# The first two feed-forward units of the second layer as eight plain block products

## The chip, the cores and the metric

The kernel runs on one core of a Trainium2 chip. The metric is device time in microseconds (us), taken as the median of several executions; one further execution was recorded by the hardware profiler, and its trace is what is read here. TensorE (PE; its weight loads are PEld) multiplies, VectorE (DVE) and ScalarE (ACT) work element by element and read TensorE's results from PSUM, GpSimd (POOL) works element by element in SBUF, SyncE (SP) issues transfers.

## The reference, cut to what matters

Two layers of a diffusion backbone run over 640 tokens of width 1024: 512 latent tokens and 128 context tokens, each group with its own conditioning vector. A layer is attention and then a feed-forward network with hidden width 2816. All is float32. The part that the change touches is the feed-forward of the second layer:

```
h = rms_norm(x, norm_ffn) * (1.0 + sc_f) + sh_f          # 640 x 1024
gate, up = jnp.split(h @ w_gate_up, 2, axis=-1)          # each 640 x 2816
x = x + g_f * ((jax.nn.silu(gate) * up) @ w_down)
```

## The kernel before

**Layout.** The residual stream is held transposed: eight tiles x0 to x7 of 128 channels by 640 tokens. A product takes weights as the stationary operand and tokens as the moving one. Each float32 operand is split into a high part of reduced precision and a low remainder (hi and lo), and `prod` sums three matmuls for each pair of blocks of 128 channels: hi x hi, hi x lo, lo x hi (L662, L663, L664). Weights are split by `split`: ACT copies the high part (L87), VectorE subtracts it (L88). They lie in four buffers each, called whi and wlo, of 1024 columns; raw weights arrive in two raw buffers of 1 MB, loaded by SP. `w_next(ahead)` gives the next piece of a list of pieces (`specs`) and prepares so many more.

**The second layer's gate and up.** Layer 1 (counted from 0) is in `FAST`. There the token columns are cut in two halves of 320 (`HALVES`), the weights of two 128-row blocks and the eight channel blocks in two each, and the 2 x 2 x 2 block product is made with seven products in place of eight (Strassen's scheme in Winograd's form). Two units, one for gate and one for up, make two hidden blocks r = 0, 1 for both token halves c = 0, 1. One unit is seven products of four channel pairs, 7 x 4 x 3 = 84 matmuls of 128 x 320. The first of the three parts (`PARTS`, 8, 8 and 6 hidden blocks) thus has four pairs of units, and the whole layer eleven. After each part, `residual` multiplies by w_down.

The seven products pair a weight factor with a token factor:

```
    FACTORS = {"A11": "B11", "A12": "B21", "S2": "T2", "S1": "T1", "S3": "T3", "A22": "T4", "S4": "B22"}
```

A11 to A22 are blocks of the weights and S1 to S4 sums of them, made by GpSimd in `fast_prep` (L496 to L499) and split into half a whi and half a wlo buffer each. B11 and B21 are the normed tokens of the first half (channel blocks 0 to 3 and 4 to 7), B12 and B22 those of the second half, T1 to T4 sums of them. B12 itself is no factor. `fast_tiles` lays the 28 pairs of tiles for the seven factors into buffers called k, q, Q and V.

**The seam.** `residual` of the attention ends with the last three output blocks for the first half, then for the second. After each half `norm_stats` makes the sums of squares (L398), `rsqrt` a chain of nine tiny VectorE steps (L99 to L105), and two sets of matmuls spread the result (rstd) over the partitions (L402, tile rb). `fast_norm` scales the eight blocks on VectorE (L456) into tmp, a P buffer of which there are three. For the first half `split` adds the shift and cuts (L90 on ACT, L91 on VectorE) into B11 and B21. For the second half ACT adds the shift (L473); then `fast_norm` goes on at once, for each i of four, with B22 and the sums T3, T1, T2, T4 on VectorE (L477 to L486), and `cut` splits each (L443 on ACT, L444 on GpSimd). `fast_unit` then evacuates the products by ACT (L534) and VectorE (L522), gate applies Silu on ACT (L558), and up multiplies on GpSimd (L562).

**Order.** The program is handed to a planner which simulates the engines and fixes each engine's order of instructions from the order in the text (earlier is more urgent), the operands' readiness and the buffers' release. On the chip each engine then goes through its own list in that order and waits where an operand is late.

Of the kernel before, what the change touches and what calls it, by code (L numbers as in the profile page):

```python
# [12 lines left out]
F32R = mybir.dt.float32r  # L13
I32 = mybir.dt.int32
AF = mybir.ActivationFunctionType
ALU = mybir.AluOpType
# [3 lines left out]
P = 128  # L20
D = 1024
KC = D // P
DEPTH = 2
SEQ = 128
DEC = 512
NT = SEQ + DEC
# [9 lines left out]
HALF = NT // 2  # L36
HALVES = ((0, HALF), (HALF, NT))
FAST = (1,)
# [8 lines left out]
class Net:  # L47
# [398 lines left out]
    def fast_norm(self, state, half, rb):  # L446

        nc = self.nc
        v = nc.vector
        l, _, T, a = state  # L450
        g0, g1 = HALVES[half]
        segs = [(s, e, c) for s, e, c in ((g0, min(g1, DEC), 0), (DEC, g1, 1)) if s < e]

        def scaled(out, k):
            for s, e, c in segs:
                v.scalar_tensor_tensor(out[:, s - g0:e - g0], self.xT[k][:, s:e], a[:, k, c:c + 1],  # L456
                                       rb[:, s - g0:e - g0], ALU.mult, ALU.mult)

        n = KC // 2
        if half == 0:  # L460
            for name, k0 in (("B11", 0), ("B21", n)):
                for i in range(n):
                    tmp = self.t([P, HALF], "P", bufs=3)
                    scaled(tmp, k0 + i)
                    self.split(*T[name][i], tmp, bias=self.m(l, 3, k0 + i, 0))
            return
        for i in range(n):
            tmp = self.t([P, 2, HALF], "P", bufs=3)
            for j, k in enumerate((i, n + i)):
                scaled(tmp[:, j], k)  # L470
                for s, e, c in segs:
                    w = tmp[:, j, s - g0:e - g0]
                    nc.scalar.activation(w, w, AF.Identity, bias=self.m(l, 3, k, c))  # L473
            b12, b22 = tmp[:, 0], tmp[:, 1]
            self.cut(T["B22"][i], b22)
            t3 = self.fast_temp()
            v.tensor_tensor(t3, b22, b12, ALU.subtract)  # L477
            self.cut(T["T3"][i], t3)
            for part in T["B11"][i]:
                v.tensor_tensor(b12, b12, part.bitcast(F32), ALU.subtract)  # L480
            self.cut(T["T1"][i], b12)
            v.tensor_tensor(b22, b22, b12, ALU.subtract)
            self.cut(T["T2"][i], b22)
            t4 = self.fast_temp()
            v.tensor_tensor(t4, T["B21"][i][0].bitcast(F32), b22, ALU.subtract)
            v.tensor_tensor(t4, t4, T["B21"][i][1].bitcast(F32), ALU.add)  # L486
            self.cut(T["T4"][i], t4)
# [56 lines left out]
        self.fast_product(p3, T)  # L544
        out(0, 1, lambda o: add(o, p3, u))

    def fast_gate_up(self, T, n, act, side):

        nc = self.nc
        for i in range(0, n, 2):  # L550
            g = [self.t([P, NT], "P", bufs=3) for _ in range(2)]

            def part(r, c):
                return g[r][:, c * HALF:(c + 1) * HALF]

            def gate(r, c, add):
                o = add(part(r, c))
                nc.scalar.activation(o, o, AF.Silu)  # L558

            def up(r, c, add):  # L560
                x, o = add(self.fast_temp()), part(r, c)
                nc.gpsimd.tensor_tensor(o, o, x, ALU.mult)  # L562

            self.fast_unit(T, gate)
            self.step(side)
            self.fast_unit(T, up)
            for r in (1, 0):
                self.split(act[0][i + r], act[1][i + r], g[r])
            self.step(side)

    def norm_chunk(self, state, k, g0, g1, rb):
# [20 lines left out]
    def wstream(self):  # L592

        ins = self.ins
        specs = []

        def spec(key, src, n, parts, shape):
            for a, b in parts:
                specs.append((key, n, src, (a, b), shape))

        every, half = slice(0, None), [slice(0, P), slice(P, 2 * P)]
        for l in range(DEPTH):
            for i in range(0 if l else 2, len(self.blocks)):
                spec(("in", l, i), ins["w_in"][l, i], KC, [(slice(4 * j, 4 * j + 4), every) for j in range(2)], [4, 256])
            for i in range(4):
                spec(("out", l, i), ins["w_out"][l, i], KC, [(every, h) for h in half], [KC, P])
            j0 = 0
            for n in PARTS:
                if l in FAST:
                    for i, name in self.fast_order(n):  # L610
                        u, j = i % 2, j0 // 2 + i // 2
                        specs.append((("gu", l, u, j), KC, ins["w_gate_up"][l, u, j], name, None))
                else:
                    for j in range(j0 // 2, (j0 + n) // 2):
                        for h in half:
                            for u in range(2):
                                spec(("gu", l, u, j), ins["w_gate_up"][l, u, j], KC, [(every, h)], [KC, P])
                for i in range(4):
                    spec(("dn", l, j0, i), ins["w_down"][l, i, :, j0:j0 + n], n, [(every, h) for h in half], [n, P])
                j0 += n  # L620
        self.specs = specs
        self.raws, self.wt, self.pos, self.prepped, self.loaded = {}, {}, 0, 0, 0
        self.spare = None
# [528 lines left out]
    def ffn(self, l, h, side):  # L1152
        nc = self.nc
        nxt = None
        for pi, n in enumerate(PARTS):
            if pi == 2:
                while side:
                    self.step(side)
            if pi < 2 or l == DEPTH - 1:
                act = [[self.t([P, NT], f"{x}{j}", F32R) for j in range(n)] for x in ("hi", "lo")]  # L1160
            else:
                v = self.t([P, 6, NT], "V", F32R)
                act = [[self.t([P, NT], "Q", F32R, bufs=6) for _ in range(n)], [v[:, j] for j in range(n)]]
            if l in FAST:
                self.fast_gate_up(h, n, act, side)
            for j in range(0 if l in FAST else n):
                out = []
                for u in range(2):
                    w = self.w_next()
                    s, parts = self.acc2()  # L1170
                    for i in range(2):
                        self.prod(parts[i], self.columns(w, h, GROUPS[i], range(KC)))
                    out.append(s)
                    if u == 0:
                        sg = self.t([P, NT], "P", bufs=3)
                        nc.scalar.activation(sg, s, AF.Silu)
                        if pi or j > SKIP:
                            self.step(side)
                nc.vector.tensor_tensor(sg, out[1], sg, ALU.mult)
                self.split(act[0][j], act[1][j], sg)  # L1180
                if pi or j > SKIP:
                    self.step(side)
            if pi == len(PARTS) - 1 and l + 1 < DEPTH:
                nxt = (l + 1, 0)
            r = self.residual(l, act, 5, range(n), nxt, side)
        return r
# [92 lines left out]
```

## Time and profile before

| | us |
|---|---|
| median of 3 executions | 1732.97 |
| lowest and highest | 1732.89 and 1733.89 |
| the profiled execution, its own time | 1731.6 |
| its span, first to last instruction | 1729.8 |
| TensorE busy in it | 1659.9 |
| VectorE, ScalarE, GpSimd busy | 1184.7, 674.7, 469.4 |

The span is what the trace shows; the 1.8 us between it and the execution's own time lie outside the instructions. Busy time of TensorE is from modelled ends of pipelined matmuls, so how many matmuls a stretch holds says more than its busy share. The granted clock of TensorE has two levels, 1.2 and 2.4 GHz; 1.00 stands for the higher one.

### The profile page before, as it was taken

What the parts mean: (1) busy time and instruction counts of PE and PEld (TensorE: products, weight loads), DVE (VectorE), ACT (ScalarE), POOL (GpSimd) and SP (SyncE); (2) the same over time, 40 slices, a digit from 0 to 9 for tenths busy, and PEclk for the clock granted to TensorE, in tenths of its full rate; (3) what the DMA queues carried; (4) which work ended last, traced back from release to release, by engine and by line L of the source; (5) the groups of instructions that cost most, each with busy time, mean ns of one, the idle gap of its engine ahead of it and who ended that gap; (6) DMA issues with size and microseconds to landing.
All of it is one profiled execution on the core that took longest, in us unless ns stands there. A gap on an engine that the chain in (4) does not pass through costs nothing.

```text
span 1729.8 us, 29420 instructions
## 1 busy us (share of the span) xinstructions
PE 1659.9 (96%) x11934; PEld 1577.7 (91%) x11934; DVE 1184.7 (68%) x2019; ACT 674.7 (39%) x1309; POOL 469.4 (27%) x410
## 2 busy tenths in 40 slices
PE   8989889999999999999999999999959999999999
PEld 6869878898999999999989998888948999999998
DVE  5786667878588978722267875777488854883672
ACT  4433376733321122212245425766244432441440
POOL 0243534400000000000003364443056622741440
PEclk9989999998999999999999999999968999999999
DMA  9343211153265655321231202112101221222222
GB/s 343 120 161 106 56 25 32 44 197 120 66 215 171 200 178 186 106 89 59 89 113 54 79 17 52 34 53 74 49 25 49 98 98 60 87 100 72 74 80 80
DMA packets 44264, 169.23 MB, mean 98 GB/s; under 512 B 5600, under 2 KB 8416, under 8 KB 32864
## 3 DMA queue, kind: packets, MB, share of 16 engines
q1 hardware_dynamic: 44128, 167.34, 29.2%
q8 instruction: 94, 1.54, 0.4%
q14 instruction: 42, 0.34, 0.1%
HBM read 152.90 MB, written 3.93 MB: 91 GB/s over the span
## 4 chain that ended last, share of the span: by engine, by line
PE 86%; DVE 6%; ACT 2%; DMA 2%; POOL 1%; issue 1%; SPq 0%; DVEq 0%; POOLq 0%; ACTq 0%
PE S L663 21%; PE S L662 21%; PE S L664 21%; PE mm L978 3%; PE S L957 3%; PE S L873 3%; PE S L874 2%; PE S L237 2%; PE mm L974 2%; PE mm L662 2%; PE mm L663 1%; PE mm L664 1%; DMA Q<-in_w_mod 1%; DVE wlo L88 1%; DVE mx L893 1%
## 5 line engine op out<-in xcount | busy, mean ns | idle before, releaser
L87 ACT ACTIVATE whi<-raw 128x512 fp32r<-128x512 f32 (+2 forms) x280 | 227.4, 829 | 612.2 <-PE S L663 511.2
L88 DVE TENSOR_TENSOR wlo<-raw,whi 128x512 fp32r<-128x512 f32 (+2 forms) x280 | 299.3, 1084 | 100.2 <-ACT whi L87 95.8
L664 PE MATMUL S<-k,wlo 128*128 128x256 f32 (+2 forms) x880 | 272.8, 310 | 0.0
L662 PE MATMUL S<-k,whi 128*128 128x256 f32 (+2 forms) x880 | 271.2, 311 | 1.4 <-ACT k L90 1.4
L663 PE MATMUL S<-lo,whi 128*128 128x384 f32 (+2 forms) x864 | 267.5, 310 | 0.0
L664 PE MATMUL S<-hi,wlo 128*128 128x384 f32 (+2 forms) x864 | 266.9, 310 | 0.0
L662 PE MATMUL S<-hi,whi 128*128 128x256 f32 (+2 forms) x864 | 266.2, 310 | 0.0
L663 PE MATMUL S<-q,whi 128*128 128x256 f32 (+2 forms) x836 | 259.8, 311 | 0.0
L1109 DVE SCALAR_TENSOR_TENSOR x<-S,modT,x 128x128 f32<-128x128 f32 (+4 forms) x137 | 66.5, 525 | 196.6 <-PE S L664 196.5
L662 PEld LDWEIGHTS S<-k,whi 128*128 128x128 f32 x880 | 166.8, 190 | 3.2 <-ACT k L90 1.9
L664 PEld LDWEIGHTS S<-k,wlo 128*128 128x128 f32 x880 | 167.6, 190 | 0.0
L663 PEld LDWEIGHTS S<-lo,whi 128*128 128x128 f32 x864 | 162.4, 188 | 1.7 <-issue 1.7
L664 PEld LDWEIGHTS S<-hi,wlo 128*128 128x128 f32 x864 | 162.5, 188 | 0.0
L662 PEld LDWEIGHTS S<-hi,whi 128*128 128x128 f32 x864 | 161.7, 188 | 0.8 <-issue 0.8
L663 PEld LDWEIGHTS S<-q,whi 128*128 128x128 f32 x836 | 158.6, 190 | 3.6 <-issue 3.4
L586 POOL TENSOR_TENSOR lo<-P,hi 128x640 fp32r<-128x640 f32 (+2 forms) x12 | 13.3, 1107 | 531.6 <-ACT hi L585 531.2
L317 DVE SCALAR_TENSOR_TENSOR Q<-V,cT,Q 128x512 f32<-128x512 f32 x224 | 152.7, 747 | 0.0
L662 PE MATMUL S<-whi,hi 128*128 128x256 f32 x512 | 147.9, 289 | 2.4 <-ACT Q L245 1.9
L893 DVE TENSOR_REDUCE mx<-S 128x1 f32<-128x768 f32 x128 | 119.5, 951 | 43.6 <-PE S L874 43.3
L664 PE MATMUL S<-whi,lo 128*128 128x256 f32 x512 | 146.5, 287 | 0.2 <-DVE lo L91 0.2
L663 PE MATMUL S<-wlo,hi 128*128 128x256 f32 x512 | 146.3, 286 | 0.0
L662 PEld LDWEIGHTS S<-whi,hi 128*128 128x128 f32 x512 | 98.7, 193 | 5.5 <-issue 2.5
(263 smaller groups left out, 3699.3 us busy)
## 6 DMA issues: line engine op xcount, KB each, us to landing
raw<-in_w_gate_up SPq DMA_DIRECT2D x44, 1024.0 KB, 4.8
V<-in_w_mod SPq DMA_DIRECT2D x64, 512.0 KB, 3.9
raw<-in_w_in SPq DMA_DIRECT2D x16, 1024.0 KB, 4.9
raw<-in_w_down SPq DMA_DIRECT2D x16, 1024.0 KB, 5.0
Q<-in_w_mod SPq DMA_DIRECT2D x32, 256.0 KB, 3.4
raw<-in_w_out SPq DMA_DIRECT2D x8, 1024.0 KB, 4.9
raw<-in_w_down SPq DMA_DIRECT2D x8, 768.0 KB, 4.2
raw<-raw SPq DMA_DIRECT2D x40, 128.0 KB, 2.2
```

The source lines that it names most:

```text
L87: nc.scalar.activation(hi, src, AF.Copy)
L88: nc.vector.tensor_tensor(lo, src, hi.bitcast(F32), ALU.subtract)
L237: nc.tensor.matmul(o, lhsT=l_[k][:, c], rhs=r_[:, w], start=k == 0 and i == 0, stop=k == KC - 1 and i == 2)
L317: ins = nc.vector.scalar_tensor_tensor(a, v, self.cT[:, k, c:c + 1], a, ALU.mult, ALU.add)
L662: self.nc.tensor.matmul(out, lhsT=lh, rhs=rh, start=(i == 0), stop=False)
L663: self.nc.tensor.matmul(out, lhsT=lh, rhs=rl, start=False, stop=False)
L664: self.nc.tensor.matmul(out, lhsT=ll, rhs=rh, start=False, stop=(i == n - 1))
L873: nc.tensor.matmul(out, lhsT=Q[j][:, cols], rhs=keys[:, k0:k0 + n], start=True, stop=False)
L893: nc.vector.tensor_reduce(mx, s[:, 0:n], AX.X, ALU.max, negate=True)
L957: nc.tensor.transpose(ps[:, i * P:(i + 1) * P], p[:, i * P:(i + 1) * P], self.ident)
L978: nc.tensor.matmul(o[64 * j:64 * j + 64], lhsT=self.V[:, v, 512 + 64 * j:576 + 64 * j], rhs=pts[j][:, i * P:(i + 1) * P], start=first, sto ...
L1109: self.nc.vector.scalar_tensor_tensor(x[:, s:e], src[:, s - a:e - a], self.m(l, which, mb, c), x[:, s:e], ALU.mult, ALU.add)
```

## The change

The first pair of units of the second layer (gate and up of hidden blocks 0 and 1) is made by `plain_units` from the eight plain block products: for each token half c, each hidden block r and each of gate and up, one sum over eight channel blocks, 24 matmuls of 128 x 320. The weights of these two units come as four whole pieces of eight blocks (1024 columns) and no longer as fourteen half pieces. `fast_norm` now cuts both B12 and B22 for the second half, leaves the uncut tiles in `self.whole` (buffers hi4 to hi7, with B12's cut in lo4 to lo7), and no longer makes the sums; the new `fast_sums`, called between the first half's products and the second half's in `plain_units`, makes T3, T1, T2 and T4 from them. The later pairs of units are as before. The activation tiles of a part are asked for a pair at a time and no longer all at the part's start.

```diff
@@ fast_norm @@
         if half == 0:
+            self.whole = {}
             for name, k0 in (("B11", 0), ("B21", n)):
...
             return
+        T["B12"] = []
         for i in range(n):
-            tmp = self.t([P, 2, HALF], "P", bufs=3)
+            tmp = self.t([P, 2, HALF], f"hi{n + i}")
+            b12 = self.t([P, NT], f"lo{n + i}", F32R)
+            T["B12"].append((b12[:, 0:HALF], b12[:, HALF:NT]))
             for j, k in enumerate((i, n + i)):
                 scaled(tmp[:, j], k)
                 for s, e, c in segs:
                     w = tmp[:, j, s - g0:e - g0]
                     nc.scalar.activation(w, w, AF.Identity, bias=self.m(l, 3, k, c))
-            b12, b22 = tmp[:, 0], tmp[:, 1]
-            self.cut(T["B22"][i], b22)
+                self.cut(T[("B12", "B22")[j]][i], tmp[:, j])
+            self.whole[i] = tmp
+
+    def fast_sums(self, T):
+
+        v = self.nc.vector
+        for i in range(KC // 2):
+            b12, b22 = self.whole[i][:, 0], self.whole[i][:, 1]
             t3 = self.fast_temp()
             v.tensor_tensor(t3, b22, b12, ALU.subtract)
             self.cut(T["T3"][i], t3)
@@ fast_gate_up @@
-    def fast_gate_up(self, T, n, act, side):
-
-        nc = self.nc
-        for i in range(0, n, 2):
+    def plain_units(self, T, act):
+
+        nc = self.nc
+        g = [self.t([P, NT], "P", bufs=3) for _ in range(2)]
+        n = KC // 2
+        rows = [(k, b, i) for i in range(n) for k, b in ((i, 0), (n + i, 1))]
+        w = [[self.w_next(1), self.w_next(1)], [self.w_next(1), self.w_next(0)]]
+        for c, names in enumerate((("B11", "B21"), ("B12", "B22"))):
+            if c == 0:
+                rows = sorted(rows)
+            else:
+                self.fast_sums(T)
+                rows = sorted(rows, key=lambda x: (x[2], x[0]))
+            for r in range(2):
+                s = self.S()
+                o = g[r][:, c * HALF:(c + 1) * HALF]
+                p = s[:, 0:HALF], s[:, 512:512 + HALF]
+                for u in range(2):
+                    hi, lo = w[r][u]
+                    self.prod(p[u], [((hi[:, k], lo[:, k]), T[names[b]][i]) for k, b, i in rows])
+                    if u == 0:
+                        nc.scalar.activation(o, p[0], AF.Silu)
+                nc.vector.tensor_tensor(o, p[1], o, ALU.mult)
+        a = act(0), act(1)
+        for r in range(2):
+            self.split(*a[r], g[r])
+
+    def fast_gate_up(self, T, n, act, side, first):
+
+        nc = self.nc
+        if first:
+            self.plain_units(T, act)
+        for i in range(2 if first else 0, n, 2):
...
             self.fast_unit(T, up)
+            a = act(i), act(i + 1)
             for r in (1, 0):
-                self.split(act[0][i + r], act[1][i + r], g[r])
+                self.split(*a[r], g[r])
@@ wstream @@
                 if l in FAST:
+                    if j0 == 0:
+                        for h in half:
+                            for u in range(2):
+                                spec(("gu", l, u, 0), ins["w_gate_up"][l, u, 0], KC, [(every, h)], [KC, P])
                     for i, name in self.fast_order(n):
                         u, j = i % 2, j0 // 2 + i // 2
+                        if j == 0:
+                            continue
@@ ffn @@
-            if pi < 2 or l == DEPTH - 1:
+            if l in FAST:
+                assert l == DEPTH - 1
+                act = [], []
+
+                def tiles(j):
+                    assert j == len(act[0])
+                    for a, x in zip(act, ("hi", "lo")):
+                        a.append(self.t([P, NT], f"{x}{j}", F32R))
+                    return act[0][j], act[1][j]
+            elif pi < 2:
...
             if l in FAST:
-                self.fast_gate_up(h, n, act, side)
+                self.fast_gate_up(h, n, tiles, side, pi == 0)
```

## Rows read from the trace of the kernel before

**Rows 1.** Profile page: span, TensorE's share, forty slices of TensorE and its clock, loads.
```profile
span 1729.8 us, 29420 instructions
...
PE 1659.9 (96%) x11934; PEld 1577.7 (91%) x11934; DVE 1184.7 (68%) x2019; ACT 674.7 (39%) x1309; POOL 469.4 (27%) x410
...
PE   8989889999999999999999999999959999999999
...
PEclk9989999998999999999999999999968999999999
...
raw<-in_w_gate_up SPq DMA_DIRECT2D x44, 1024.0 KB, 4.8
```
**Rows 2.** Stretches: length, busy time (instructions) by engine, granted clock, DMA share, GB/s.
```profile
1261.40:1307.00 45.60, 23.32 (x76) 16.72 (x75) 44.15 (x79) 22.77 (x54) 31.65 (x27) 0.55 0.07 24
1307.00:1729.80 422.80, 418.63 (x2849) 418.31 (x2847) 274.51 (x393) 148.09 (x256) 168.17 (x126) 1.00 0.24 82
```
**Rows 3.** The seam's stretch for TensorE's lines L662, L663 and L664, in turn.
```profile
1261.40:1307.00 45.60, 10.21 (x21) 0.55 0.07 24
1261.40:1307.00 45.60, 9.81 (x18) 0.55 0.07 24
1261.40:1307.00 45.60, 8.09 (x19) 0.55 0.07 24
```
**Rows 4.** A stretch behind the seam, in the columns of group 2.
```profile
1310.00:1350.00 40.00, 40.00 (x275) 40.00 (x274) 34.12 (x49) 19.97 (x38) 24.35 (x18) 1.00 0.23 79
```
**Rows 5.** TensorE's timeline in the seam: start, length, instruction, idle time before it.
```profile
1263.27 0.42 PE L662 MATMUL S<-k,whi 128*128 128x320 f32 x1 [1.24 <-ACT k L90]
...
1281.30 1.51 PE L402 MATMUL mm<-ident,rstd 128*128 128x128 f32 x6 [4.05 <-DVE rstd L105]
...
1305.25 0.47 PE L662 MATMUL S<-k,whi 128*128 128x320 f32 x1
1305.52 0.47 PE L663 MATMUL S<-k,whi 128*128 128x320 f32 x1
```
**Rows 6.** VectorE's groups from 1261.4 to 1281.3: busy us, mean ns, idle time before.
```profile
L91 DVE SCALAR_TENSOR_TENSOR k<-P,modT,k 128x320 fp32r<-128x320 f32 x8 | 7.3, 932 | 0.0
L88 DVE TENSOR_TENSOR wlo<-raw,whi 128x512 fp32r<-128x512 f32 x7 | 4.7, 682 | 0.0
...
L101 DVE TENSOR_SCALAR rs_c<-rs_b 128x3 int32<-128x3 int32 x1 | 1.2, 1232 | 0.0
```
**Rows 7.** VectorE's timeline in the seam: start, length, instruction.
```profile
1262.08 1.46 DVE L456 SCALAR_TENSOR_TENSOR P<-x,A,mm 128x320 f32<-128x320 f32 x3
...
1275.49 0.54 DVE L91 SCALAR_TENSOR_TENSOR k<-P,modT,k 128x320 fp32r<-128x320 f32 x1
...
1281.00 0.15 DVE L105 SCALAR_TENSOR_TENSOR rstd<-rs_b,rs_c 128x3 f32<-128x3 f32 x1
...
1307.73 1.05 DVE L486 TENSOR_TENSOR Q<-Q,k 128x320 f32<-128x320 f32 x1
```
**Rows 8.** VectorE's groups from 1281 to 1311, one of the five lines of sums.
```profile
L480 DVE TENSOR_TENSOR P<-P,k 128x320 f32<-128x320 f32 x8 | 7.3, 942 | 0.1
```
**Rows 9.** GpSimd's timeline in the seam: weight sums (L496 to L498) and cuts (L444).
```profile
1278.81 1.65 POOL L498 TENSOR_TENSOR raw<-PT,raw 128x512 f32<-128x512 f32 x1 [6.38 <-DVE wlo L88]
...
1284.08 1.27 POOL L496 TENSOR_TENSOR PT<-raw 128x512 f32<-128x512 f32 x1 [1.11 <-DMA raw<-in_w_gate_up]
1285.53 0.88 POOL L444 TENSOR_TENSOR k<-P,k 128x320 fp32r<-128x320 f32 x1 [0.18 <-ACT k L443]
1286.35 1.63 POOL L497 TENSOR_TENSOR raw<-raw 128x512 f32<-128x512 f32 x1
...
1309.48 0.87 POOL L444 TENSOR_TENSOR V<-Q,V 128x320 fp32r<-128x320 f32 x1
```
**Rows 10.** VectorE's groups from 1190 to 1245, the split of a whole weight piece.
```profile
L88 DVE TENSOR_TENSOR wlo<-raw,whi 128x1024 fp32r<-128x1024 f32 x8 | 9.7, 1219 | 1.5 <-PE mm L978 1.5
```
**Rows 11.** Waits from 1307 to the end: who waited for whom, us in total, times, longest.
```profile
ACT hi L87 <- POOL P L562: 20.1, 18, 4.0
```

## The prediction

> **What bounds the kernel now.** I read the page first, then stretches of time around the one place where the page shows a hole. TensorE is busy 96% of the span, so the rest of the kernel leaves little, but one of the forty slices stands at five tenths, and the clock row falls to 6 in the same place [rows 1]. That slice is the seam between the second layer's output projection and its feed-forward. The stretches show it: the 45.6 us from 1261.4 hold 76 TensorE instructions at a granted clock of 0.55, while the 422.8 us behind them are full at 1.00 [rows 2]. Of the 76, 21 + 18 + 19 = 58 are products (the three lines of prod) [rows 3]; the others make the norm's statistics. A full stretch does 275 products of 320 columns in 40 us, 0.1455 us each [rows 4]. So the seam could hold 45.6 / 0.1455 = 313 products and holds 58: the 255 missing are worth 37.1 us, and since TensorE is full to the end afterwards, all of that stands in the time.
>
> Why it is empty is read from the TensorE timeline and then from the engines that release it. The first feed-forward product starts at 1263.27, the statistics of the second token half are spread at 1281.30 after a wait of 4.05, and 128x320 products come singly, behind ACT or POOL, until 1305; even there they go at 0.267 us, the 1.2 GHz level [rows 5]. VectorE is the engine behind this. From 1262 to 1281 it norms the first half (eight scalings, eight subtractions at 0.93 us mean), splits weight pieces and drops the rstd chain between them (one tiny integer step took 1.23 us) [rows 6]; the last subtraction starts at 1275.49, rstd at 1281.00 and the last of the 24 token sums at 1307.73 [rows 7, 8]. GpSimd's first cut starts at 1285.53, its last ends at 1309.48 + 0.87 = 1310.35 [rows 9]. TensorE lacks operands, not time: five of the seven fast products need a sum or a block of the second half.
>
> **The change, part by part.** Times below are on the clock of the trace of before.
>
> *More products.* Two fast units are 2 x 7 x 4 x 3 = 168 matmuls, eight plain products 8 x 8 x 3 = 192, of the same 320 columns: 24 x 0.1455 = 3.5 us more.
>
> *Products that need no sum.* The first four (first token half) need only B11 and B21: 96 matmuls, 14.0 us at full clock, against 24 in the old order. VectorE makes the eight tiles in 8 x 0.46 for the scalings (three in 1.46 [rows 7]) and 8 x 0.46 to 8 x 0.93 for the subtractions [rows 6], 7.4 to 11.1 us. Each tile feeds 12 matmuls = 1.75 us, more than one tile costs VectorE, so TensorE is the slower one once the first subtraction is out, near 1264.5. They last to about 1279 to 1281.
>
> *Weights.* Fourteen splits of 512 columns and eight GpSimd sums become four splits of 1024, at 1.22 us on VectorE [rows 10]. All four live at once in the four whi and four wlo buffers; the projection's last three pieces hold three of them. The first goes where the old pair went, the second and third fit in VectorE's idle time before 1261 as those pieces end, the fourth falls into the norm: I charge VectorE 2.4 us for two. The seven splits that stood there before (0.68 each [rows 6], 4.8 us) go, and with them 1.2 us in which VectorE stood at one tiny step behind GpSimd. rstd then comes at 1281.1 - 4.8 - 1.2 + 2.4 = 1277.5. The next raw tile is freed as the third piece is split and a load lands in 4.8 us [rows 1], so GpSimd's weight sums for the next unit still fall on the norm, a few microseconds later than now.
>
> *Second half.* B12 and B22 are cut in full: four cuts more, 24 instead of 20. In before the first cut came 4.4 us after rstd (1285.53 against 1281.15), so now at 1282.0; a cut beside VectorE's sums takes 1.1 us, the pitch of the old 20 (24.8 us with two weight sums of 1.27 and 1.63 among them [rows 9]), so a pair is out each 2.2 us: 1284.2 to 1290.8. A pair feeds 24 matmuls, 3.5 us, so the second four products run 1284.2 to 1298.2. TensorE stands about 3 to 5 us before them. The buffers called hi and lo 4 to 7 that now hold these tiles are the projection's operands, free at 1261.4 when its last product ends: no wait, as the rb that the scalings need is far later. The old queue for three P buffers goes too. The evacuations lie under products and get fewer: four Silu as before, and four multiplications from PSUM for fourteen additions and four products on GpSimd.
>
> *The sums, made meanwhile.* From 1282.0, 24.8 us as before plus 4 x 1.1, less none to 2.9 us for the weight sums that may be made earlier: the last cut ends at 1308 to 1311. The next fast unit (84 matmuls) has 36 that need no sum and 36 more that need only the first three rows of sums. Between 1298.2 and 1307.0 TensorE has room for 60. The gate's first split waits for a whi buffer, hence for the first of the four second-half products, and then queues behind VectorE's sums. That cost is not in the trace of before, where those splits lay elsewhere; its bounds are none of the 60 done and all of them. I take 30: the 36 need only two or three splits, and VectorE's queue is what they stand in.
>
> *The sum.* By 1307.0 TensorE has done 192 + 30 = 222 products instead of 58. Less the 24 that are extra, it is 222 - 58 - 24 = 140 ahead, x 0.1455 = 20.4 us. Bounds: with none of the 60 and 5 us more of stall (34 matmuls), 76 ahead, 11 us; with all 60, 170 ahead, 24.7 us; with TensorE full from 1264.5 on, 292 done, 210 ahead, 30.6 us. The profiled execution took 1731.6 for its span of 1729.8; 20.4 less is 1711.2. The median, 1732.97, gives 1712.6, and I forecast 1713.
>
> *Moves that I cost at nothing.* The activation tiles are now asked for pair by pair, behind the pair's products, instead of all at a part's start. Cover: their splits already wait on GpSimd, not on a buffer (20.1 us over 18 waits, none of it TensorE's [rows 11]). If that cover went, it would be paid ten times, once for each later pair.
>
> **The rivals.**
> - *The sums are the next stall.* GpSimd gets more to do, and cuts and VectorE's sums alternate at 1.1 us a pair instead of overlapping (alone a cut is 0.87 [rows 9], a sum ran 0.94 mean [rows 8]). If the next units' weight sums (4 x 1.4) and seven splits (4.8) also take turns with them, the last cut ends at 1282.0 + 26.4 + 5.6 + 4.8 = 1318.8; some 21 products of the gate are left then, 3 us, so it ends at 1321.9. The old kernel ends that gate at 1307.0 + (252 - 58) x 0.1455 = 1335.2: 13.3 us gained, 1720. For it: both engines are full there. Against: the weight sums can be made while VectorE still works on the first half. The Trainium skill (SBUF — State Buffer, "SBUF: two separate sides") says that a VectorE instruction with two SBUF inputs and a GpSimd one that reads SBUF hold a port pair by turns, for a whole instruction. The subtractions at 0.93 us beside GpSimd and 0.54 without it [rows 6, 7] agree (GpSimd had then been idle for 6.38 [rows 9]); by the page's rule this rival's 1720 would hold.
> - *The clock stays low.* The first products again come tile by tile, in an order fixed by the planner, and TensorE stays at 0.267 us: 96 x 0.267 = 25.6, to 1290; the second four end 6 us later: 14 gained, 1719. For it: the clock fell in just this place [rows 2, 5]. Against: twelve products a tile in place of three.
> - *TensorE is fed at once.* All 60, and rstd some microseconds earlier: 25 to 30 us, 1703 to 1708.
> - *Nothing changes* (within 0.2%, 3.5 us, about what a measurement of this kernel can tell from no change): the plain units' end and the sums both slip by some 17 us more, for example if the four whole pieces are split only behind the second norm.
> - *Slower.* The splits of each pair's result come late, as their tiles are asked for late; the three P buffers then hold up the next pair's evacuation and TensorE stands once per pair. It decides from 20.4 / 10 = 2.0 us a pair; at 3 us it gives 1743. Against it: the full stretches after 1307 [rows 2, 4], where that chain has slack now.
>
> **How the numbers follow.** Chances: forecast (1708 to 1718) 0.55; fed at once 0.08; sums as next stall 0.14; low clock 0.10; no change 0.05; slower 0.08. Faster by over 0.2%: 0.55 + 0.08 + 0.14 + 0.10 = 0.87. The range runs from 1704 (29 us, near the top bound) to 1725 (the rival at 1720 with 5 us of further stall); outside lie no change, slower and a few hundredths at the fast end.
>
> **What would show each step.** Right: the slice at five tenths becomes eight or nine; in the 45.6 us from the projection's end some 220 products and a granted clock over 0.8; rstd at 16 us after that end instead of 20; a TensorE wait of 3 to 5 us ahead of the second-half products, and another behind them on a split or a cut; 24 cuts ending near 1308; a full TensorE from then on. Wrong: fewer than 150 products in that window, clock near 0.55 (low clock), last cut behind 1315 (sums), or any repeated TensorE wait behind 1320 (slower).

## The result and the profile after

| | median us (runs) | lowest to highest |
|---|---|---|
| before | 1733.89 (5) | 1732.89 to 1739.64 |
| after | 1722.33 (5) | 1716.69 to 1724.14 |

The ratio is 0.9924, with a 95% interval of 0.99 to 0.9948: 11.6 us faster where 20.4 were forecast. The profiled execution of after took 1722.35 us for a span of 1720.3.

One thing has to be taken out before the traces can be laid side by side. Up to some 20 us before the end of the output projection both programs issue the same instructions in the same order on every engine, and yet the first spread of rstd (L402), the first thing behind the output projection, starts at 1261.26 in the trace of before and at 1265.65 in that of after; in the other traces it lies between 1260.8 and 1268.3. The 4.39 us between before and after arose long before the change: one and the same ScalarE instruction of the attention starts at 1188.44 and at 1192.83. So below, a point of the seam is given as +us behind that spread, and **the length from the spread to the end of the span** stands for what a kernel does from the seam on: 1729.8 - 1261.26 = 468.5 before, 1720.3 - 1265.65 = 454.65 after, 13.9 less.

The page of after, the rows that answer to [rows 1]:

```profile
span 1720.3 us, 29417 instructions
...
PE 1657.2 (96%) x11958; PEld 1577.8 (92%) x11958; DVE 1178.0 (68%) x1999; ACT 671.5 (39%) x1301; POOL 457.8 (27%) x402
...
PE   8989899999999999999999998999998999999999
...
PEclk8989999999999999999999999999998999999999
```

The five is gone from the TensorE slices, and TensorE has 24 more instructions, as forecast. The stretch that answers to [rows 2], of the same 45.6 us from +0.14, and the one behind it:

```profile
1265.79:1311.39 45.60, 33.15 (x193) 30.56 (x192) 44.26 (x76) 22.86 (x56) 29.29 (x26) 0.85 0.12 46
1311.39:1720.30 408.91, 404.76 (x2756) 404.44 (x2754) 264.47 (x375) 142.60 (x244) 158.24 (x119) 1.00 0.23 82
```

And its products, lines L711, L712 and L713 in turn, against [rows 3]:

```profile
1265.79:1311.39 45.60, 19.00 (x59) 12.09 (x59) 0.85 0.12 46
1265.79:1311.39 45.60, 19.93 (x58) 12.23 (x59) 0.85 0.12 46
1265.79:1311.39 45.60, 18.62 (x58) 11.82 (x57) 0.85 0.12 46
```

That is 59 + 58 + 58 = 175 products where before had 58 (each count holds one product of the projection, which reaches into the window). Less the 24 extra ones, 93 ahead, x 0.1455 = 13.5 us, close to the 13.9 of the lengths. TensorE is full behind the seam in both kernels, so the whole gain, and the whole shortfall against the forecast's 222, lies in these 45.6 us. The waits of TensorE in after, from the seam to the end, show what they hold now. Of the waits of [rows 5], the 4.05 ahead of the second spread is gone; the 1.24 ahead of the first product is still there:

```profile
PE S L711 <- ACT whi L87: 8.0, 1, 8.0
PE S L712 <- DVE k L91: 1.3, 2, 0.9
PE mm L398 <- DVE PT L364: 1.3, 1, 1.3
```

The long one, on TensorE's timeline (the second spread now follows without a wait):

```profile
1281.12 0.85 PE L402 MATMUL mm<-ident,rstd 128*128 128x128 f32 x6
...
1295.93 0.41 PE L712 MATMUL S<-q,whi 128*128 128x320 f32 x1 [0.44 <-POOL q L444]
...
1296.47 0.30 PE L713 MATMUL S<-q,wlo 128*128 128x320 f32 x1
1304.79 0.63 PE L711 MATMUL S<-k,whi 128*128 128x320 f32 x1 [8.01 <-ACT whi L87]
```

The instruction that ends the wait is the first product of the next unit. The planner put it in TensorE's list ahead of the plain up products of the second half; those wait for Silu, which stands behind the same copies on ScalarE. What ScalarE does meanwhile (start, length, instruction, idle time before it and who ended it):

```profile
1298.40 0.47 ACT L443 ACTIVATE q<-Q 128x320 fp32r<-128x320 f32 x1 [2.74 <-DVE Q L487]
1299.47 0.47 ACT L443 ACTIVATE q<-hi 128x320 fp32r<-128x320 f32 x1 [0.60 <-DVE hi L490]
1301.60 0.47 ACT L443 ACTIVATE V<-hi 128x320 fp32r<-128x320 f32 x1 [1.67 <-DVE hi L492]
1301.98 0.45 ACT L443 ACTIVATE Q<-hi 128x320 fp32r<-128x320 f32 x1
1303.75 0.47 ACT L443 ACTIVATE V<-hi 128x320 fp32r<-128x320 f32 x1 [1.31 <-DVE hi L492]
1304.12 1.13 ACT L87 ACTIVATE whi<-raw 128x512 fp32r<-128x512 f32 x2
1305.16 0.42 ACT L581 ACTIVATE P<-S 128x320 f32<-128x320 f32 x1
```

ScalarE is idle for 5.2 of these 8.0 us. It goes through its list in order, and the weight splits (L87, two of them in the row above; TensorE needs the first) and the Silu (L581) stand behind five copies of token sums, four of which waited for VectorE. VectorE and GpSimd, in the same time:

```profile
1302.57 1.14 DVE L492 TENSOR_TENSOR hi<-hi 128x320 f32<-128x320 f32 x1
1303.64 1.15 DVE L495 TENSOR_TENSOR Q<-k,hi 128x320 f32<-128x320 f32 x1
1304.71 1.16 DVE L490 TENSOR_TENSOR hi<-hi,k 128x320 f32<-128x320 f32 x1
1305.79 0.48 DVE L495 TENSOR_TENSOR Q<-k,hi 128x320 f32<-128x320 f32 x1
1306.19 0.48 DVE L496 TENSOR_TENSOR Q<-Q,k 128x320 f32<-128x320 f32 x1
```

```profile
1302.26 1.10 POOL L444 TENSOR_TENSOR V<-hi,V 128x320 fp32r<-128x320 f32 x1
1303.33 1.10 POOL L444 TENSOR_TENSOR Q<-hi,Q 128x320 fp32r<-128x320 f32 x1
1304.40 1.12 POOL L444 TENSOR_TENSOR V<-hi,V 128x320 fp32r<-128x320 f32 x1
1307.75 1.46 POOL L508 TENSOR_TENSOR raw<-PT,raw 128x512 f32<-128x512 f32 x1 [2.23 <-DVE wlo L88]
```

As long as GpSimd has cuts to make, both engines start one instruction each 1.07 us. At 1305.52 GpSimd runs out of them, and from there the same sums are 0.40 apart. The Trainium skill (SBUF — State Buffer, "SBUF: two separate sides") says that a VectorE instruction with two SBUF inputs and a GpSimd one that reads SBUF hold a shared port pair one at a time, each for a whole instruction. The trace agrees in the main: 1.07 for a pair, where a sum alone takes 0.40 from start to start and a cut alone 0.87 [rows 9]. The pair is 0.2 shorter than these two added, so a part of them does overlap.

### The profile page after: what moved, and what is told of

The parts are those of the page before. It is cut to its first block, busy times and chain, and to the rows that moved or that the text cites. A ratio compares the mean times of both kernels' runs of the same rounds, so it can differ in the third digit from the quotient of the medians.

```text
span 1720.3 us, 29417 instructions
## 1 busy us (share of the span) xinstructions
PE 1657.2 (96%) x11958; PEld 1577.8 (92%) x11958; DVE 1178.0 (68%) x1999; ACT 671.5 (39%) x1301; POOL 457.8 (27%) x402
## 4 chain that ended last, share of the span: by engine, by line
PE 84%; DVE 7%; ACT 3%; DMA 2%; POOL 2%; issue 2%; SPq 0%; POOLq 0%; DVEq 0%; ACTq 0%
PE S L712 21%; PE S L711 21%; PE S L713 21%; PE S L1006 3%; PE mm L1027 3%; PE S L922 3%; PE S L923 2%; PE mm L1023 2%; PE S L237 2%; PE mm L711 1%; PE mm L712 1%; PE mm L713 1%; DMA Q<-in_w_mod 1%; DVE wlo L88 1%; DVE mx L942 1%
## 5 line engine op out<-in xcount | busy, mean ns | idle before, releaser
L87 ACT ACTIVATE whi<-raw 128x1024 fp32r<-128x1024 f32 (+2 forms) x272 | 224.6, 842 | 617.4 <-PE S L712 526.6
L88 DVE TENSOR_TENSOR wlo<-raw,whi 128x1024 fp32r<-128x1024 f32 (+2 forms) x272 | 302.4, 1127 | 100.2 <-ACT whi L87 95.9
L711 PE MATMUL S<-k,whi 128*128 128x256 f32 (+2 forms) x904 | 277.5, 310 | 9.3 <-ACT whi L87 8.0
L713 PE MATMUL S<-k,wlo 128*128 128x256 f32 (+2 forms) x904 | 279.2, 309 | 0.0
L712 PE MATMUL S<-lo,whi 128*128 128x256 f32 (+2 forms) x880 | 272.7, 310 | 0.0
L713 PE MATMUL S<-hi,wlo 128*128 128x384 f32 (+2 forms) x864 | 266.9, 310 | 0.0
L711 PE MATMUL S<-hi,whi 128*128 128x256 f32 (+2 forms) x864 | 266.2, 310 | 0.0
L712 PE MATMUL S<-q,whi 128*128 128x256 f32 (+2 forms) x832 | 257.6, 310 | 0.4 <-POOL q L444 0.4
L711 PEld LDWEIGHTS S<-k,whi 128*128 128x128 f32 x904 | 170.6, 190 | 10.9 <-ACT whi L87 8.3
L713 PEld LDWEIGHTS S<-k,wlo 128*128 128x128 f32 x904 | 171.0, 189 | 0.0
L712 PEld LDWEIGHTS S<-lo,whi 128*128 128x128 f32 x880 | 165.7, 188 | 1.7 <-issue 1.7
L713 PEld LDWEIGHTS S<-hi,wlo 128*128 128x128 f32 x864 | 162.5, 188 | 0.0
L711 PEld LDWEIGHTS S<-hi,whi 128*128 128x128 f32 x864 | 161.7, 188 | 0.8 <-issue 0.8
L712 PEld LDWEIGHTS S<-q,whi 128*128 128x128 f32 x832 | 157.0, 189 | 4.1 <-issue 3.4
L711 PE MATMUL S<-whi,hi 128*128 128x256 f32 x512 | 146.8, 287 | 2.4 <-ACT Q L245 1.9
L713 PE MATMUL S<-whi,lo 128*128 128x256 f32 x512 | 145.9, 286 | 0.0
L712 PE MATMUL S<-wlo,hi 128*128 128x256 f32 x512 | 145.5, 284 | 0.0
L711 PEld LDWEIGHTS S<-whi,hi 128*128 128x128 f32 x512 | 97.5, 190 | 5.5 <-issue 2.5
```

The source lines that it names most:

```text
L87: nc.scalar.activation(hi, src, AF.Copy)
L88: nc.vector.tensor_tensor(lo, src, hi.bitcast(F32), ALU.subtract)
L711: self.nc.tensor.matmul(out, lhsT=lh, rhs=rh, start=(i == 0), stop=False)
L712: self.nc.tensor.matmul(out, lhsT=lh, rhs=rl, start=False, stop=False)
L713: self.nc.tensor.matmul(out, lhsT=ll, rhs=rh, start=False, stop=(i == n - 1))
```

## The experiments

The first theories, of where the forecast's missing 7 us went. **A**: the order of the products; gate and up of a hidden block share one PSUM tile S, so that the up products could not run in the norm's time. **B**: the token sums and ScalarE's list behind them; then a better order of products moves nothing. All lengths are from the first spread to the end of the span; each ratio is to executions of before taken together with that kernel's.

| kernel | median us (runs) | ratio to before, 95% | first spread | length |
|---|---|---|---|---|
| silu_behind_both | 1725.68 (7) | 0.996 (0.9945 to 0.9975) | 1266.95 | 460.15 |
| own_psum_tiles | 1720.76 (6) | 0.993 (0.9914 to 0.9946) | 1261.05 | 455.85 |
| no_sums | 1707.5 (4) | 0.9857 (0.9836 to 0.9877) | 1260.83 | 444.27 |
| buffers_alone | 1736.77 (10) | 1.0023 (1.0011 to 1.0035) | 1260.82 | 471.8 |
| after_again | 1720.83 (1) | | 1262.37 | 456.43 |
| sums_behind_split | 1717.92 (5) | 0.9911 (0.9896 to 0.9927) | 1261.97 | 453.33 |
| sums_behind_split_own_tiles | 1718.43 (6) | 0.9911 (0.9896 to 0.9927) | 1266.43 | 453.17 |
| three_rows_behind | 1720.07 (4) | 0.9916 (0.9897 to 0.9936) | 1268.34 | 454.56 |
| cuts_on_vector | 1717.14 (5) | 0.9903 (0.9889 to 0.9918) | 1265.17 | 448.93 |
| cuts_on_vector_own_tiles | 1711.93 (4) | 0.9871 (0.9855 to 0.9887) | 1260.82 | 448.58 |
| cuts_on_vector_split_first | 1712.51 (4) | 0.9876 (0.9862 to 0.989) | 1260.80 | 448.9 |
| before_cuts_on_vector | 1733.28 (12) | 1.0001 (0.9988 to 1.0013) | 1266.65 | 468.65 |

**silu_behind_both.** In `plain_units` of after:

```diff
-                    if u == 0:
-                        nc.scalar.activation(o, p[0], AF.Silu)
+                nc.scalar.activation(o, p[0], AF.Silu)
```

> The changed kernel with one line moved: Silu of the gate product is written behind both products of a hidden block, not between them. The measure is the stretch from the start of the first rstd spread (the end of the output projection) to the end of the span: 468.5 us before, 454.6 after the change. Theory A: gate and up of a block share one PSUM tile, and the up product is held behind Silu, which stands in ScalarE's queue behind cuts of the sums; so 48 products of the second half run only behind the 8 us wait. Then they now run ahead of it: 48 x 0.1455 = 7 us less, 446 to 449. Theory B: TensorE would wait for the sums and the next weights anyway and the wait only grows by what is moved: 452 to 455.

Theory A fell, and the length, 460.15, is above the range of either. The up products did move: all 192 plain products are done before the wait on the split, which is now 1.56 long, and still nothing is gained. The planner put some of them ahead of the second rstd spread, so the second norm began at +19.0 instead of +16.4. The split that TensorE needs starts at +43.8, behind a copy for which ScalarE stood idle for 3.89 until its sum came. A later split is late too, and this one not by a sum: it stands on ScalarE behind the split of the plain units' own result, and TensorE waits 4.58 for it at +55.5. So this run doesn't tell the sums from the rest of ScalarE's list; no_sums below does.

```profile
1310.37 0.47 ACT L443 ACTIVATE V<-Q 128x320 fp32r<-128x320 f32 x1 [3.89 <-DVE Q L496]
1310.74 1.14 ACT L87 ACTIVATE whi<-raw 128x512 fp32r<-128x512 f32 x2
```

```profile
1322.48 0.41 PE L710 MATMUL S<-Q,whi 128*128 128x320 f32 x1 [4.58 <-ACT whi L87]
```

**own_psum_tiles.** A tile S for each of gate and up, the Silu left where it is in after:

```diff
-                s = self.S()
...
-                p = s[:, 0:HALF], s[:, 512:512 + HALF]
+                p = []
                 for u in range(2):
+                    p.append(self.S()[:, 0:HALF])
```

> The changed kernel with gate and up of a block in two PSUM tiles of their own. Same stretch, 454.6 in the changed kernel. Theory A: three of the four first-half products can run tile by tile in the norm's window, 72 instead of 48 products before the second rstd spread, and no up product waits for Silu: 444 to 448, up to 3 us below the run with Silu moved. Theory B: 452 to 455. A third possibility: three PSUM tiles for four products make the fourth wait for an evacuation on VectorE, which is full there: 450 to 454.

TensorE does 60 plain products before the second spread (48 in after, 72 expected) and 168 before its long wait (144), and gives all of it back: the wait is 10.03 instead of 8.01 and ends at +43.1 instead of +39.1, now for the Silu in ScalarE's list. Length 455.85, between the two profiles of after (454.65 and 456.43) and 0.85 above theory B's range: theory A fell.

```profile
1304.17 0.63 PE L711 MATMUL S<-lo,whi 128*128 128x320 f32 x1 [10.03 <-ACT P L581]
```

**no_sums.** The sums alone taken out:

```diff
-                self.fast_sums(T)
+                T["T1"], T["T2"], T["T3"], T["T4"] = T["B11"], T["B21"], T["B22"], T["B22"]
```

> The changed kernel without the four token sums: T1 to T4 are other blocks of the tokens, so 24 VectorE instructions, 16 copies on ScalarE and 16 subtractions on GpSimd are left out and all products stay. Theory A with the sums as the throttle of ScalarE's queue: the 8 us wait and the slow clock behind it (about 2 us) go, 444 to 446. If the wait is for a weight buffer or a split as such, it stays: 452 to 455.

444.27, as expected. The wait on the split is 0.3. With 24 sums, 16 copies and 16 cuts out of the way the length is 10.4 to 12.2 us shorter than in the two profiles of after; that bounds what any better order or pace of the sums can bring with this order of products.

```profile
PE S L711 <- ACT whi L87: 0.3, 1, 0.3
```

**buffers_alone.** Before, with two moves to which the prediction gave no cost, the tiles in hi4 to hi7 and the late asking:

```diff
-            tmp = self.t([P, 2, HALF], "P", bufs=3)
+            tmp = self.t([P, 2, HALF], f"hi{n + i}")
...
+            a = act(i), act(i + 1)
             for r in (1, 0):
-                self.split(act[0][i + r], act[1][i + r], g[r])
+                self.split(*a[r], g[r])
...
```

> The kernel before with two side parts of the change alone: the second half's uncut tiles lie in the buffers hi4 to hi7 and not in three P buffers, and the activation tiles are asked for a pair at a time. Forecast: the tiles cost nothing and the longer buffers save at most the 2 us in which the fourth pair waited for a P buffer: 466 to 468.5 from the first rstd spread to the end (468.5 before). If asking late holds up the pairs: above 470.

A miss: 471.8, 3.3 longer than before, and slower by 0.23%. That is above 470, but not for the reason given there. By the trace, asking late for the activation tiles is not it: from +46 on TensorE is busy throughout, as in before. The loss is in the seam (the two moves were not run apart). All eight scalings now run at once (4.75 us on VectorE, 3.59 before the first sums in the trace of before), and an evacuation of the first fast unit stands behind the sums, with TensorE waiting 4.4 for it:

```profile
PE S L663 <- ACT q L443: 4.6, 1, 4.6
PE S L663 <- DVE P L522: 4.4, 1, 4.4
```

Two further theories for ScalarE's list. **C**: only the order is wrong; put the split ahead of the copies and the wait is gone. **D**: the pace of the sums sets the end, wherever the split stands.

**sums_behind_split**, **sums_behind_split_own_tiles**, **three_rows_behind** and **after_again.** `fast_sums` takes a range of rows; two rows (in the third kernel one) come where all four did, the others behind the second half's products:

```diff
-                self.fast_sums(T)
+                self.fast_sums(T, range(2))
...
-                        nc.scalar.activation(o, p[0], AF.Silu)
+                        last = nc.scalar.activation(o, p[0], AF.Silu)
                 nc.vector.tensor_tensor(o, p[1], o, ALU.mult)
+        self.w_prep(self.pos + 2)
+        with self.tc.issue_after(last.ins):
+            self.fast_sums(T, range(2, n))
```

> Rows 0 and 1 of the token sums stay where they are; rows 2 and 3 go behind the second-half products, and the next unit's first two weight splits (A11, A12) are planned between, so that on ScalarE these splits and the Silu of the second half stand ahead of the copies for rows 2 and 3. Length counted: from the second layer's last projection's first rstd spread to the span's end (454.65 in the changed kernel). Theory C (the 8 us wait is ScalarE's order: the split is ready but stands behind copies that wait for VectorE; the sums themselves come in time): 447 to 450, the wait on the split falls to under 2 us and no new one of over 3 us takes its place; time 1714 to 1718. Theory D (the pace of the sums is the bound wherever the split stands): the wait moves to a later product that needs a sum of rows 2 or 3, 453 or more, time 1720 to 1724.

> As sums_behind_split, and gate and up of a hidden block in PSUM tiles of their own as in own_psum_tiles (455.85 counted from the rstd spread). Theory C: both stalls go, 444 to 448, near the 444.3 of the run without sums; time 1710 to 1716. Theory D: 453 or more, with TensorE waiting on a sum's split or cut; time 1720 or more.

> As sums_behind_split, but only row 0 of the sums ahead and rows 1 to 3 behind the split. Theory C with sums that come in time: 446 to 450, no worse than sums_behind_split. If the sums' pace is the bound once they start late, this one is longer than sums_behind_split by up to the 6 us in which one row's sums are made (four pairs of about 1.1 us and the copies): 452 to 458, with TensorE waiting on a cut of GpSimd.

> The changed kernel once more, for its second profile: the wait on the split at the seam should be 8 us again and the length from the rstd spread to the end within 1 us of 454.65, while the time of the rstd spread itself, which comes from the start of the program, may differ by some 4 us (1265.65 in the first profile, 1260.8 to 1266.95 in the runs since).

Theory C fell, mostly. In sums_behind_split the wait on the split shrinks from 8.0 to 4.5, not under 2, and the length by 1.3 to 3.1 us to 453.33, theory D's range; the two rows that stay ahead are late enough to hold the split. Its time, 1717.92, is in C's range, and the later wait that D expected did not come, so this run fits neither in full. With own tiles (453.17) TensorE waits 7.00 for the Silu, which no theory named. With three rows behind, the wait on the split is gone (0.3) and a wait on a cut stands in its place:

```profile
PE S L715 <- POOL V L444: 5.9, 2, 4.9
...
PE S L714 <- ACT whi L87: 0.3, 1, 0.3
```

That is theory D: 454.56. The second profile of after (after_again) repeats the 8.0 us wait, but its length is 456.43, 1.8 more than the first profile of after and more than I had allowed; 1.2 of it is there by the second spread (+16.7 against +15.5), where the single products of the norm's time ran at 0.267 in two spells instead of one. So differences of a length under some 2 us tell nothing.

Then the pace itself. **E**: it is the turns of VectorE and GpSimd. **F**: it is VectorE's list, whoever makes the cuts.

**cuts_on_vector** (and the same edit on two of the kernels above). `cut` gets an engine, and the sums' 16 cuts go to VectorE (T1, T2 and T4 as T3):

```diff
-    def cut(self, pair, src):
+    def cut(self, pair, src, e=None):
...
-        self.nc.gpsimd.tensor_tensor(lo, src, hi.bitcast(F32), ALU.subtract)
+        (e or self.nc.gpsimd).tensor_tensor(lo, src, hi.bitcast(F32), ALU.subtract)
...
-            self.cut(T["T3"][i], t3)
+            self.cut(T["T3"][i], t3, v)
...
```

> The changed kernel with the 16 low-part subtractions of the token sums on VectorE instead of GpSimd; the eight of B12 and B22 stay on GpSimd. In the changed kernel's trace a sum on VectorE takes 0.48 (starts 0.40 apart) when GpSimd is idle and a cut 0.87, but from +21 to +39 after the rstd spread both start one pair each 1.08. Theory E (the two engines take turns, and that pace is what makes the sums and all that queues behind them late): 24 sums and 16 cuts at 0.40 are 16 us behind the scalings, so the last cut ends near +39 to +42 instead of +49, the sums in that stretch are at 0.48 once GpSimd's eight are done, the 8 us wait falls under 3, and the length from the spread to the end is 446 to 450 (454.65 and 456.43 in the two profiles of the changed kernel); time 1713 to 1717. Rival F (VectorE's queue itself is the pace: cuts that wait there for ScalarE's copies hold up the sums behind them): last cut +47 or later, 453 or more, time 1720 or more.

> As cuts_on_vector, and gate and up of a hidden block in PSUM tiles of their own as in own_psum_tiles (455.85). Theory E: 444 to 449, the earlier products of the norm window now count because the sums come in time for them; time 1710 to 1716. Rival F: 453 or more.

> As sums_behind_split_own_tiles (453.17), with the 16 cuts of the sums on VectorE. Theory E: 444 to 448, close to the 444.3 without any sums; time 1709 to 1715. Rival F: 452 or more, as before.

Theory E held in the length: 448.93, 5.7 to 7.5 less than after, with 16 more instructions on VectorE. The same edit on own_psum_tiles and on sums_behind_split_own_tiles takes off 7.3 and 4.3. The median, 1717.14, is 0.14 above the range of E, and its interval overlaps that of after, so here the length alone shows the gain; for the other two kernels the intervals with and without the edit lie apart. TensorE's wait on the split is 2.68 long and ends at +33.1, in after 8.01 long and at +39.1. On VectorE's timeline the sums go at the old pitch until GpSimd has made its eight cuts, and then sums and cuts at 0.40:

```profile
1291.33 2.25 DVE L487 TENSOR_TENSOR Q<-hi 128x320 f32<-128x320 f32 x2
1293.51 0.48 DVE L444 TENSOR_TENSOR q<-Q,q 128x320 fp32r<-128x320 f32 x1
1293.91 0.48 DVE L496 TENSOR_TENSOR Q<-Q,k 128x320 f32<-128x320 f32 x1
```

```profile
1298.28 0.42 PE L711 MATMUL S<-k,whi 128*128 128x320 f32 x1 [2.68 <-ACT whi L87]
```

The products in the 45.6 us from +0.14, in the counting of [rows 3]: 76 + 76 + 75 = 227.

```profile
1265.31:1310.91 45.60, 23.43 (x76) 14.47 (x76) 0.96 0.12 44
1265.31:1310.91 45.60, 24.35 (x76) 14.95 (x76) 0.96 0.12 44
1265.31:1310.91 45.60, 23.33 (x75) 14.60 (x75) 0.96 0.12 44
```

The date of the last cut was a miss: +49.0, not +39 to +42 (rival F had +47 or later). VectorE's list has the next units' weight splits between the last sums, and TensorE waits for none of these cuts for more than 0.8. cuts_on_vector_own_tiles has the same length (448.58) and has the lowest median of the kernels that leave nothing out, 1711.93 us; its interval lies below that of after. Why its median is 5.2 below that of cuts_on_vector, with ranges that don't meet (1708.93 to 1713.73 against 1715.67 to 1718.38), the seam doesn't explain: the profiles differ by 4.35 in the time of the first spread and by 0.35 behind it, and the 4.35 is there by 1190 us already, where both still run the same instructions. That stays open. cuts_on_vector_split_first (448.9) missed its 444 to 448: with the pace mended, the other place of the sums adds nothing that a length can tell, and TensorE still waits 2.90 for the Silu.

**before_cuts_on_vector.** The same edit on the kernel before, as a control:

> The kernel before, with the 16 low-part subtractions of T1 to T4 on VectorE instead of GpSimd, and the four of B22 left on GpSimd; no plain products. It tells whether the turns of the two engines were already the price of the old seam, which holds five products fed by sums. Theory E: the 20 cuts and 24 sums that went at 1.08 a pair take 40 x 0.40 = 16 us for the moved part, so the last cut ends some 5 to 8 us earlier than +49 after the rstd spread, and the length from the spread to the end is 460 to 464 (468.5 before); time 1724 to 1729. Rival G (the old seam is set by the order in which the singles come and by its P buffers, not by the cuts' pace): 467 or more, time 1731 to 1735.

No change (468.65), and rival G's number; the last cut ends at +49.8, no earlier. VectorE made the moved cuts at 0.40 there too, but the last of the four cuts of B22, which were left on GpSimd, did not get in between: it took 5.42 instead of 0.87, and TensorE waited for it.

```profile
1303.22 5.42 POOL L444 TENSOR_TENSOR q<-P,q 128x320 fp32r<-128x320 f32 x1 [7.68 <-ACT q L443]
```

```profile
1308.69 0.63 PE L663 MATMUL mm<-q,whi 128*128 128x320 f32 x1 [4.41 <-POOL q L444]
```

So the moved cuts gained only together with the plain products, which give the sums some time. Whether it is the order of the old seam (G) or this one held cut that ate the gain there, no run separates: all 20 cuts on VectorE were not tried.

## Why the prediction was right and where it was not

The sign, the place and the range were right, the forecast's size was not: 13.9 us by the lengths and 11.6 by the medians against 20.4. The 1722.33 lies above the 1708 to 1718 that had most of the chance, in the part of the range that stood there for the rival at 1720.

- **More products, full TensorE behind the seam, a freed P queue, tiles asked late.** 24 instructions more; no repeated wait behind the seam, so the rival "slower" fell. But two moves without a cost in the prediction, the tiles in hi4 to hi7 and the late asking, lengthen the old kernel by 3.3 us (buffers_alone). In after no wait of TensorE shows either of them; no run has the change without them.
- **rstd and the second half.** rstd came at 1280.81, +15.2 (forecast +16.2); the first cut at +18.3 (+20.7); the last of the eight cuts of B12 and B22 ended at +30.2 (+29.5), and TensorE waited 0.44 for it; the last cut of all at 1314.8, +49.2 (+47 to +50). The weights' part of the working stands. The wait of 3 to 5 us ahead of the second-half products did not come: half of the first four products filled it.
- **The first four products tile by tile: failed.** Only 48 of the 96 ran before the second spread, the gates of both hidden blocks; up shares its gate's PSUM tile and was planned behind it and its Silu (with tiles of their own it was 60). They ended at +23.2, not +18 to +20. own_psum_tiles suggests that this cost nothing by itself: with 24 more products done ahead of the long wait, the wait ended 4.0 us later.
- **30 of 60 products of the next unit while the sums are made: failed, and this is the term that missed.** By the end of the 45.6 us the 175 were 5 of these, 169 of the 192 plain ones and one of the projection: 47 short of 222, x 0.1455 = 6.8 us, so 13.6 left of 20.4. The prediction put the gate's first split into VectorE's queue. It stood in ScalarE's, where it needs no sum itself but lies behind copies that do, and the second half's Silu with it: 8.01 us of wait, 55 products' worth. no_sums takes the wait away (444.27), cuts_on_vector most of it (448.93): with all the work still there it reaches 227 products where 222 were forecast, and is 19.6 us shorter than before where 20.4 were. So what the sum lacked is the way, through ScalarE's list, by which the pace of the turns reaches TensorE; for the cuts themselves it had that pace right.
- **The rivals.** "The sums are the next stall" gave 1720 and came nearest to the 1722.33, with the right engines and the wrong path: the last cut came at +49.2, as the forecast had it, and not at this rival's +57.5, and the sums' pace reached TensorE through ScalarE's list. That the number is so near is partly luck. That the two engines hold each other up, on which the prediction hung that rival's time, is borne out by cuts_on_vector. "The clock stays low" was a small part: 0.66 in one stretch of 5 us of the norm's time and 0.50 in the 5 us of the long wait; the products behind that wait ran at 0.267 for 4 us. The clock fell while TensorE stood still, and in no_sums, without the wait, it stays at 1.00 there, so it is a consequence. "Fed at once" (1703 to 1708) is where no_sums lies, 1707.5, but with the sums left out; with them no kernel here got so far.

## What to carry to other kernels

A sum that is not on the critical path can still set the end, if its copies stand in the in-order list of an engine that also feeds the critical one: read that engine's idle time with its releasers, not its busy share (ScalarE was idle for 5.2 of the 8.0 us in which TensorE stood still for a split of 0.6). Where VectorE and GpSimd both run float32 work on two SBUF operands, count it as one queue: in turns a sum and a cut took 1.07, on VectorE alone 2 x 0.40, and 16 subtractions moved from the less busy to the busier engine made the seam 5.7 to 7.5 us shorter. It has to be tried in the kernel at hand: on the old order the same edit gained nothing. And when independent work has been added to cover a chain, take the chain out once: the 10.4 us of no_sums told in one run how much was left to win, and that it lay with the sums.

## What was not expected of the hardware

The turns are not always fair. With cuts on both engines each got every second turn (fourteen pairs in a row in after, 1.08 us each). Once VectorE had a run of sums and cuts at 0.40 one behind the other, a GpSimd instruction that had started waited through nine to eleven of them: 5.42 us for a cut of 0.87 in before_cuts_on_vector, 5.49 for a weight sum (L508; 1.46 in after) in cuts_on_vector. What ended these waits can be read: within 80 us behind the first spread the traces hold eight GpSimd instructions of over 2.3 us, and in seven of them GpSimd got through with the first VectorE instruction that had one of its operands in PSUM (L522, L532 or L582); in the eighth VectorE's next instruction came 0.1 us later than usual. In before_cuts_on_vector the held cut ended at 1308.64:

```profile
1307.43 0.48 DVE L480 TENSOR_TENSOR P<-P,k 128x320 f32<-128x320 f32 x1
1307.84 0.48 DVE L522 TENSOR_TENSOR P<-S,Q 128x320 f32<-128x320 f32 x1
1308.24 0.75 DVE L486 TENSOR_TENSOR Q<-Q,k 128x320 f32<-128x320 f32 x1
```

What decides whether the two take turns or VectorE keeps going, no run here tells apart.

The first rstd spread came anywhere from 1260.8 to 1268.3 in fourteen traces of kernels whose instructions are the same up to the last pieces of the projection; a few microseconds of a time can be of that kind, which is why the lengths were used.
